# Sharing the quadrant moves of every pair between ScalarE and GpSimd, with 31 regular transfers in place of 39

## The chip, the cores and the metric

The kernel runs on one core of one Trainium2 chip. The metric is device time in microseconds (us) of that core. Most executions of one kernel agree within 0.3%, so every timed run stands beside runs of the kernel before on the same chip. Ratios are the mean time of one kernel's fast runs over that of the other's in the same rounds, so they are not quite the ratio of the medians quoted with them.

## The reference

```python
x:         16 x 512 x 1024 float32        weight: 1024 x 768 float32
add_value: 16 x 512 x 768  float32        scale:  0.1
out = (scale * np.matmul(x, weight) + add_value).astype(np.float32)
```

In tiles of 128 rows there are 64 tiles. One tile moves 4 KiB per partition of x in, 3 KiB of the add in and 3 KiB of the result out. With 3.1 MB of weights that is 87.03 MB in all.

## The kernel before

Tile t's rows are interleaved, so that 8 tiles of one partition are one contiguous run in memory: a transfer of 8 tiles of x is 128 rows of 32,768 bytes, one of the add or the result 128 rows of 24,576 bytes. SyncE issues all transfers in the order of a list. `x` loads tiles into 16 slots, `a` loads the add into 32 slots, `o` stores from those same slots, `w` loads weights; `l` and `r` are the two halves of tile 63.

```python
STREAM = [
    ("x", 0, 3), ("w", 0, 2), ("w", 2, 2), ("w", 4, 2), ("x", 3, 1), ("w", 6, 2),
    ("a", 0, 3), ("x", 4, 4), ("a", 3, 1), ("a", 4, 4), ("x", 8, 4), ("x", 12, 4),
    ("x", 16, 4), ("a", 8, 8), ("x", 20, 4), ("x", 24, 8), ("o", 0, 8), ("a", 16, 8),
    ("x", 32, 8), ("a", 24, 8), ("a", 32, 8), ("x", 40, 8), ("o", 8, 8), ("x", 48, 8),
    ("a", 40, 8), ("o", 16, 8), ("x", 56, 8), ("a", 48, 8), ("o", 24, 8), ("o", 32, 8),
    ("a", 56, 8), ("o", 40, 8), ("o", 48, 8), ("o", 56, 4), ("o", 60, 1), ("o", 61, 1),
    ("o", 62, 1), ("l", 63, 1), ("r", 63, 1),
]
```

x must be transposed for the product. The first 14 tiles and the last four are transposed by TensorE. A pair of the tiles in between is cast and moved between quadrants of 32 partitions in 16 small copies, and VectorE's stream transpose then finishes it. ScalarE does all 16 copies of one pair while GpSimd does those of the next; each has its own pool of two buffers.

```python
def move_pair(t0, a):                       # called for a = 0..3, four steps in a row
    act = t0 in MOVED_ACT
    if a == 0:
        if act:
            va = va_pool.tile([P, 2 * KC, 4, 64], bf16, tag="va")
        else:
            va = vp_pool.tile([P, 2 * KC, 4, 64], bf16, tag="vp")
        ...
    for b in range(4):
        move = nc.scalar.copy if act else nc.gpsimd.tensor_copy
        move(moved[t0][32 * b:32 * b + 32, :, a, :], src[32 * a:32 * a + 32, :, b, :])

def step():                                 # one tile
    ...
        for a in range(4):                  # in the middle of the tile's matmuls
            if in_pair.get(t + 8 - a) == t + 8 - a:
                move_pair(t + 8 - a, a)
    ...
    finish(t, BOTH[0], 0, N)                # VectorE: scale * product + add, into the add's slot
    if in_pair.get(t + 4) == t + 4:
        turn_moved(t + 4)                   # VectorE: stream transpose of a moved pair
```

An x slot is free for the next load only when its tile has been moved. And VectorE takes its work in program order.

Of the kernel before, what the change touches and what calls it, by code (L numbers as in the profile page):

```python
# [10 lines left out]

STREAM = [
    ("x", 0, 3), ("w", 0, 2), ("w", 2, 2), ("w", 4, 2), ("x", 3, 1), ("w", 6, 2),
    ("a", 0, 3), ("x", 4, 4), ("a", 3, 1), ("a", 4, 4), ("x", 8, 4), ("x", 12, 4),
    ("x", 16, 4), ("a", 8, 8), ("x", 20, 4), ("x", 24, 8), ("o", 0, 8), ("a", 16, 8),
    ("x", 32, 8), ("a", 24, 8), ("a", 32, 8), ("x", 40, 8), ("o", 8, 8), ("x", 48, 8),
    ("a", 40, 8), ("o", 16, 8), ("x", 56, 8), ("a", 48, 8), ("o", 24, 8), ("o", 32, 8),
    ("a", 56, 8), ("o", 40, 8), ("o", 48, 8), ("o", 56, 4), ("o", 60, 1), ("o", 61, 1),
    ("o", 62, 1), ("l", 63, 1), ("r", 63, 1),
]  # L20

X_SLOTS = 16
# [3 lines left out]
EARLY = 3  # L26



MOVED_ACT = [14, 18, 22, 26, 30, 34, 38, 42, 46, 50, 54, 58]  # L30
MOVED_POOL = [16, 20, 24, 28, 32, 36, 40, 44, 48, 52, 56]


@with_exitstack
def kernel(
# [8 lines left out]
    nc = tc.nc  # L44
    P = 128
    bf16 = mybir.dt.bfloat16
# [9 lines left out]
    KC = K // (2 * P)  # L56
# [8 lines left out]
    def rows(view, s, n):  # L65
        assert s // G == (s + n - 1) // G
        return view[:, s // G, s % G:s % G + n, :]


    w_v = weight.rearrange("(c p r) n -> p c r n", p=P, r=2)  # L70

    const = ctx.enter_context(tc.tile_pool(name="const", bufs=1))
    xb_pool = ctx.enter_context(tc.tile_pool(name="xb_pool", bufs=XB_BUFS))
    xt_pool = ctx.enter_context(tc.tile_pool(name="xt_pool", bufs=3))
    va_pool = ctx.enter_context(tc.tile_pool(name="va_pool", bufs=2))
    vp_pool = ctx.enter_context(tc.tile_pool(name="vp_pool", bufs=2))
    tp_pool = ctx.enter_context(
        tc.tile_pool(name="tp_pool", bufs=2, space=bass.MemoryType.PSUM))
    mm_pool = ctx.enter_context(
# [6 lines left out]
    ao = const.tile([P, A_SLOTS, N], fp32, name="ao")  # L86
    w_bf = const.tile([P, KJ, N], bf16, name="w_bf")

    xb_tiles, xt_tiles, mm_tiles, done = {}, {}, {}, {"cast": 0, "step": 0, "x": 0}
    in_pair = {t0 + i: t0 for t0 in MOVED_ACT + MOVED_POOL for i in range(2)}  # L90
    moved, cast_pairs = {}, set()

    def load_w(j, n):

        s = A_SLOTS - KJ + j
        if n == 1:
            nc.sync.dma_start(ao[:, s, :], w_v[:, j // 2, j % 2, :])
        else:
            nc.sync.dma_start(ao[:, s:s + 2, :], w_v[:, j // 2, :, :])  # L99
        for i in range(n):  # L100
            nc.vector.tensor_copy(w_bf[:, j + i, :], ao[:, s + i, :])  # L101

    def move_pair(t0, a):


        act = t0 in MOVED_ACT
        if a == 0:
            if act:
                va = va_pool.tile([P, 2 * KC, 4, 64], bf16, tag="va")
            else:  # L110
                va = vp_pool.tile([P, 2 * KC, 4, 64], bf16, tag="vp")
            moved[t0] = va
        k = t0 % X_SLOTS
        assert k + 1 < X_SLOTS
        src = xs[:, k:k + 2, :].rearrange("p i (c b k) -> p (i c) b k", b=4, k=64)
        for b in range(4):
            move = nc.scalar.copy if act else nc.gpsimd.tensor_copy
            move(moved[t0][32 * b:32 * b + 32, :, a, :], src[32 * a:32 * a + 32, :, b, :])  # L118
        if a == 3:
            cast_pairs.add(t0)  # L120

    def turn_moved(t0):
        xt = xt_pool.tile([P, 2, KC, P], fp32, tag="xt")
        for i in range(2):
            xt_tiles[t0 + i] = xt[:, i, :, :]
        nc.vector.transpose(  # L126
            xt.rearrange("p i c m -> p (i c m)"),
            moved.pop(t0).bitcast(fp32).rearrange("p c a k -> p (c a k)"))

    def cast_to(t):  # L130
        while done["cast"] <= t:
            i = done["cast"]
            if i in in_pair:
                assert in_pair[i] in cast_pairs
                done["cast"] += 1
                continue
            if len(xb_tiles) == XB_BUFS:
                break
            xb = xb_pool.tile([P, K], bf16, tag="xb")
            src = xs[:, i % X_SLOTS, :]  # L140
            if i < EARLY:
                nc.vector.tensor_copy(xb[:, 0:K // 2], src[:, 0:K // 2])  # L142
                other = nc.gpsimd.tensor_copy if i else nc.scalar.copy
                other(xb[:, K // 2:K], src[:, K // 2:K])  # L144
            else:
                nc.gpsimd.tensor_copy(xb, src)  # L146
            xb_tiles[i] = xb
            done["cast"] += 1

    def transpose(t, pieces=1):  # L150
        cast_to(t)

        pairs = xb_tiles.pop(t).bitcast(fp32)
        tp = tp_pool.tile([P, KC, P], fp32, tag="tp")
        for c in range(KC):
            nc.tensor.transpose(tp[:, c, :], pairs[:, c * P:(c + 1) * P], identity)  # L156
        if t % 2 == 0:
            xt = xt_pool.tile([P, 2, KC, P], fp32, tag="xt")
            for i in range(2):
                xt_tiles[t + i] = xt[:, i, :, :]  # L160
        q = KC // pieces
        evacuate = nc.scalar.copy if t <= EARLY or t > LAST_PAIR else nc.vector.tensor_copy
        for c in range(0, KC, q):
            evacuate(  # L164
                xt_tiles[t][:, c:c + q, :].bitcast(bf16), tp[:, c:c + q, :].bitcast(bf16))
# [5 lines left out]
    def product(t, j, cols):  # L171
        if (t, cols[0]) not in mm_tiles:
            mm = mm_pool.tile([P, 1024], fp32, tag="mm")
            for part in cols:
                mm_tiles[t, part] = mm
        for n0, n1 in cols:
            nc.tensor.matmul(  # L177
                mm_tiles[t, cols[0]][:, n0:n1], lhs(t, j), w_bf[:, j, n0:n1],
                start=(j == 0), stop=(j == KJ - 1))
# [3 lines left out]
    def finish(t, part, n0, n1):  # L183
        a = ao[:, t % A_SLOTS, n0:n1]
        nc.vector.scalar_tensor_tensor(  # L185
            a, mm_tiles[t, part][:, n0:n1], float(scale), a,
            op0=mybir.AluOpType.mult, op1=mybir.AluOpType.add)
# [27 lines left out]
                        op0=mybir.AluOpType.mult)  # L215
            done["step"] = EARLY

    LAST_PAIR = max(in_pair)
    EARLY_AT = A_SLOTS - KJ - EARLY

    def step():
        t = done["step"]
        if t < T - 1:
            for j in range(KJ):
                if j == KJ // 2:
                    if t + 1 not in in_pair:
                        transpose(t + 1)
                    cast_to(min(t + AHEAD, done["x"] - 1))
                    for a in range(4):
                        if in_pair.get(t + 8 - a) == t + 8 - a:  # L230
                            move_pair(t + 8 - a, a)
                product(t, j, BOTH)
            finish(t, BOTH[0], 0, N)
            if in_pair.get(t + 4) == t + 4:
                turn_moved(t + 4)
        else:
            for cols in BOTH:
                for j in range(KJ):
                    product(t, j, [cols])
                finish(t, cols, *cols)  # L240
        done["step"] += 1

    def added(t):
        assert done["step"] >= EARLY
        nc.vector.tensor_add(  # L245
            ao[:, t, :], ao[:, EARLY_AT + t, :], ao[:, t, :])

    for op, s, n in STREAM:
        last = s + n - 1
        if op == "w":  # L250
            load_w(s, n)
            head(op, s, n)
        elif op == "x":
            if last >= X_SLOTS:
                while done["cast"] <= last - X_SLOTS:
                    step()
            k = s % X_SLOTS
            nc.sync.dma_start(xs[:, k:k + n, :], rows(x_v, s, n))  # L258
            done["x"] = s + n
            if last < EARLY:  # L260
                head(op, s, n)
        elif op == "a":
            k = s % A_SLOTS
            nc.sync.dma_start(ao[:, k:k + n, :], rows(add_v, s, n))  # L264
            for t in range(s, min(s + n, EARLY)):
                added(t)
        else:
            while done["step"] <= last:
                step()
            k = s % A_SLOTS  # L270
            n0, n1 = {"o": (0, N), "l": (0, CUT), "r": (CUT, N)}[op]
            nc.sync.dma_start(rows(out_v, s, n)[:, :, n0:n1], ao[:, k:k + n, n0:n1])  # L272
# [35 lines left out]
```

## Time and profile before

| | before |
|---|---|
| time, median | 210.12 us (210.09 to 210.5, 3 runs) |
| span of the profiled run | 208.5 us |
| pairs moved, tiles transposed by TensorE | 23, 18 |

The DMA row of the page says whether the 16 DMA engines had work in each of 40 slices.

### The profile page before, as it was taken

The numbers are of one execution on the slowest core, as the hardware profiler recorded it, in microseconds if no ns is written. First come the engines' busy times: TensorE is split into PE (matmuls) and PEld (weight loads), VectorE is DVE, ScalarE is ACT, GpSimd is POOL, SyncE is SP. The second block draws the span as 40 slices with busy tenths as digits, with TensorE's granted clock in tenths as the row PEclk, the third lists the DMA queues.
The fourth block names the chain that finished last, engine by engine and source line by source line (L and its number), as shares of the span: only waits on it lengthen the run. The fifth ranks groups of instructions, "written<-read, shape, count | busy, mean of one in ns | idle before, by whom it ended". The sixth has DMA issues, their size and how long they took to land.

```text
span 208.5 us, 2886 instructions
## 1 busy us (share of the span) xinstructions
PE 181.6 (87%) x1096; PEld 110.7 (53%) x1096; DVE 101.3 (49%) x111; ACT 129.0 (62%) x206; POOL 124.3 (60%) x199
## 2 busy tenths in 40 slices
PE   0599399980899997999999999999999999989960
PEld 0455256650466664566666666666666666656630
DVE  0536535511466514855655555555553685233330
ACT  2423000499959798599999999999999900003210
POOL 1310524379898980999998899999999960001000
PEclk9999889996589999999999999999999999999997
DMA  6999999999999999999999999999999999999995
GB/s 236 415 428 440 413 429 434 421 450 406 454 418 448 407 429 462 404 443 420 442 434 413 461 418 424 420 429 437 421 434 424 432 439 424 429 418 439 429 394 214
DMA packets 5629, 87.21 MB, mean 418 GB/s; under 512 B 624, under 2 KB 752, under 8 KB 2032
## 3 DMA queue, kind: packets, MB, share of 16 engines
q1 hardware_dynamic: 5616, 87.03, 98.2%
q8 instruction: 8, 0.13, 0.3%
q14 instruction: 5, 0.04, 0.0%
HBM read 61.87 MB, written 25.17 MB: 417 GB/s over the span
## 4 chain that ended last, share of the span: by engine, by line
DMA 75%; ACT 9%; PE 7%; DVE 3%; SPq 1%; issue 1%; DVEq 0%
DMA out_dram<-ao 35%; DMA ao<-in_add_value_dram 22%; DMA xs<-in_x_dram 13%; ACT va L118 9%; PE mm L177 6%; DMA ao<-in_weight_dram 5%; DVE ao L185 2%; DVE xt L126 1%; PE tp L156 1%; SPq L258 1%; SPq L99 0%; SPq L264 0%; SPq L272 0%; DVEq L185 0%
## 5 line engine op out<-in xcount | busy, mean ns | idle before, releaser
L177 PE MATMUL mm<-w_bf,xt 128*128 128x256 bf16 (+1 forms) x1024 | 173.8, 331 | 8.8 <-DVE xt L164 6.6
L177 PEld LDWEIGHTS <-xt 128*128 128x128 bf16 x1024 | 101.3, 99 | 76.9 <-DVE xt L164 7.0
L118 ACT CAST va<-xs 32x512 bf16<-32x512 f32 x192 | 118.2, 616 | 28.8 <-DMA xs<-in_x_dram 19.1
L118 POOL CAST va<-xs 32x512 bf16<-32x512 f32 x176 | 106.8, 607 | 15.9 <-DVE xt L126 6.2
L185 DVE SCALAR_TENSOR_TENSOR ao<-mm,ao 128x768 f32<-128x768 f32 (+2 forms) x62 | 58.1, 942 | 78.1 <-PE mm L177 49.1
L146 POOL CAST xb<-xs 128x1024 bf16<-128x1024 f32 x15 | 15.2, 1040 | 43.4 <-PE tp L156 22.5
L164 ACT COPY xt<-tp 128x512 bf16<-128x512 bf16 (+1 forms) x11 | 8.2, 785 | 35.3 <-PE tp L156 35.3
L126 DVE STREAM_TRANSPOSE xt<-va 128x1024 f32<-128x1024 f32 x23 | 28.4, 1234 | 0.0
L156 PE MATMUL tp<-identity,xb 128*128 128x128 f32 x72 | 12.9, 314 | 11.2 <-DVE xb L142 7.4
L156 PEld LDWEIGHTS tp<-identity,xb 128*128 128x128 f32 x72 | 9.8, 161 | 13.7 <-issue 7.6
L164 DVE COPY xt<-tp 128x1024 bf16<-128x1024 bf16 x10 | 6.9, 686 | 10.1 <-PE tp L156 10.1
L101 DVE CAST w_bf<-ao 128x768 bf16<-128x768 f32 x8 | 4.1, 556 | 3.8 <-DMA ao<-in_weight_dram 3.8
L142 DVE CAST xb<-xs 128x512 bf16<-128x512 f32 x3 | 1.9, 696 | 6.8 <-DMA xs<-in_x_dram 6.8
L144 POOL CAST xb<-xs 128x512 bf16<-128x512 f32 x2 | 1.6, 834 | 5.5 <-DMA xs<-in_x_dram 5.5
L144 ACT CAST xb<-xs 128x512 bf16<-128x512 f32 x1 | 0.6, 618 | 4.8 <-DMA xs<-in_x_dram 4.8
L213 DVE TENSOR_SCALAR ao<-mm 128x768 f32<-128x768 f32 x2 | 1.8, 952 | 1.9 <-PE mm L177 1.9
L245 DVE TENSOR_TENSOR ao<-ao 128x768 f32<-128x768 f32 x3 | 2.7, 951 | 0.0
L144 ACT ACT_TABLE_LOAD x1 | 1.3, 1283 | 0.7 <-PEq L289 0.7
L210 ACT ACTIVATE ao<-mm 128x768 f32<-128x768 f32 x1 | 0.8, 817 | 0.0
masks.py:197 POOL MEMSET identity<- 128x128 f32 x1 | 0.2, 204 | 0.3 <-POOLq L289 0.3
masks.py:199 POOL TENSOR_SCALAR_AFFINE_SELECT identity<-identity 128x128 f32<-128x128 f32 x1 | 0.3, 292 | 0.1
L289 POOL MEMSET const-float32-0.0<- 128x1 f32 x1 | 0.1, 98 | 0.2 <-issue 0.2
(3 smaller groups left out, 0.3 us busy)
## 6 DMA issues: line engine op xcount, KB each, us to landing
ao<-in_add_value_dram SPq DMA_DIRECT2D x7, 3072.0 KB, 26.1
out_dram<-ao SPq DMA_DIRECT2D x7, 3072.0 KB, 23.9
xs<-in_x_dram SPq DMA_DIRECT2D x5, 4096.0 KB, 18.8
xs<-in_x_dram SPq DMA_DIRECT2D x5, 2048.0 KB, 26.6
ao<-in_weight_dram SPq DMA_DIRECT2D x4, 768.0 KB, 9.6
xs<-in_x_dram SPq DMA_DIRECT2D x1, 1536.0 KB, 6.1
ao<-in_add_value_dram SPq DMA_DIRECT2D x1, 1536.0 KB, 19.3
out_dram<-ao SPq DMA_DIRECT2D x1, 1536.0 KB, 12.9
```

The lines of the kernel that those rows point to most:

```text
L101: nc.vector.tensor_copy(w_bf[:, j + i, :], ao[:, s + i, :])
L118: move(moved[t0][32 * b:32 * b + 32, :, a, :], src[32 * a:32 * a + 32, :, b, :])
L126: nc.vector.transpose(xt.rearrange("p i c m -> p (i c m)"), moved.pop(t0).bitcast(fp32).rearrange("p c a k -> p (c a k)"))
L142: nc.vector.tensor_copy(xb[:, 0:K // 2], src[:, 0:K // 2])
L144: other(xb[:, K // 2:K], src[:, K // 2:K])
L146: nc.gpsimd.tensor_copy(xb, src)
L156: nc.tensor.transpose(tp[:, c, :], pairs[:, c * P:(c + 1) * P], identity)
L164: evacuate(xt_tiles[t][:, c:c + q, :].bitcast(bf16), tp[:, c:c + q, :].bitcast(bf16))
L177: nc.tensor.matmul(mm_tiles[t, cols[0]][:, n0:n1], lhs(t, j), w_bf[:, j, n0:n1], start=(j == 0), stop=(j == KJ - 1))
L185: nc.vector.scalar_tensor_tensor(a, mm_tiles[t, part][:, n0:n1], float(scale), a, op0=mybir.AluOpType.mult, op1=mybir.AluOpType.add)
L245: nc.vector.tensor_add(ao[:, t, :], ao[:, EARLY_AT + t, :], ao[:, t, :])
L258: nc.sync.dma_start(xs[:, k:k + n, :], rows(x_v, s, n))
```

## The change

Its intent: fewer and larger transfers in a regular order (31, in eights from tile 8 on), each issued well ahead; and to make that possible, moves with half the latency, shared by ScalarE and GpSimd within every pair from tile 14 on. The diff, cut to its core:

```diff
 STREAM = [
     ("x", 0, 3), ("w", 0, 2), ("w", 2, 2), ("w", 4, 2), ("x", 3, 1), ("w", 6, 2),
-    ("a", 0, 3), ("x", 4, 4), ("a", 3, 1), ... ("o", 56, 4), ("o", 60, 1), ("o", 61, 1),
-    ("o", 62, 1), ("l", 63, 1), ("r", 63, 1),
+    ("a", 0, 8), ("x", 4, 4), ("x", 8, 8), ("a", 8, 8), ("x", 16, 8), ("o", 0, 8),
+    ("a", 16, 8), ("x", 24, 8), ("a", 24, 8), ("o", 8, 8), ("x", 32, 8), ("a", 32, 8),
+    ("x", 40, 8), ("o", 16, 8), ("a", 40, 8), ("x", 48, 8), ("a", 48, 8), ("o", 24, 8),
+    ("x", 56, 8), ("o", 32, 8), ("a", 56, 8), ("o", 40, 8), ("o", 48, 8), ("o", 56, 6),
+    ("o", 62, 2),
 ]
-MOVED_ACT = [14, 18, 22, ... 58]
-MOVED_POOL = [16, 20, 24, ... 56]
+MOVED = [14, 16, 18, ... 60, 62]
-    vp_pool = ctx.enter_context(tc.tile_pool(name="vp_pool", bufs=2))
     ...
+    def move_pair(t0, half):
+        if half == 0:
+            va = va_pool.tile([P, 2 * KC, 4, 64], bf16, tag="va")
         for b in range(4):
+            for a, move in ((2 * half, nc.scalar.copy), (2 * half + 1, nc.gpsimd.tensor_copy)):
+                move(moved[t0][32 * b:32 * b + 32, :, a, :],
+                     src[32 * a:32 * a + 32, :, b, :])
     ...
-                    for a in range(4):
-                        if in_pair.get(t + 8 - a) == t + 8 - a:
-                            move_pair(t + 8 - a, a)
+                    for half in range(2):
+                        if in_pair.get(t + 6 - half) == t + 6 - half:
+                            move_pair(t + 6 - half, half)
```

## The prediction

> **What bounds the kernel now.** I read the page from the bottom of part 3 upwards: first what the transfers do, then how deep their queue is, and only then the engines.
>
> ```profile
> span 208.5 us, 2886 instructions
> PE 181.6 (87%) x1096; PEld 110.7 (53%) x1096; DVE 101.3 (49%) x111; ACT 129.0 (62%) x206; POOL 124.3 (60%) x199
> ...
> DMA  6999999999999999999999999999999999999995
> ...
> q1 hardware_dynamic: 5616, 87.03, 98.2%
> ...
> HBM read 61.87 MB, written 25.17 MB: 417 GB/s over the span
> ```
>
> The DMA row is 9 in 38 of 40 slices, and the queue that carries the data took 98.2% of 16 engines' span. The inputs and the output together are 87.03 MB; nothing is moved twice. So the kernel stands at the time that 87.03 MB need, plus a start and an end. The stretches say how much that is:
>
> ```profile
> 0.00:2.00 2.00, 0.00 (x0) 0.00 (x0) 0.00 (x0) 1.27 (x1) 0.70 (x6) 1.00 0.36 68
> 2.00:205.00 203.00, 181.63 (x1096) 110.67 (x1096) 101.26 (x111) 127.78 (x206) 123.61 (x193) 0.97 1.00 427
> 205.00:208.50 3.50, 0.00 (x0) 0.00 (x0) 0.00 (x0) 0.00 (x0) 0.00 (x0) 0.58 0.31 118
> ```
>
> The last two columns are DMA share and GB/s. From 2 to 205 us the share is 1.00 at 427 GB/s: no hole is left to fill. The records of single packets give the same: the first data packet starts at 1.75 us, the last ends at 207.27 us, and of these 205.5 us each of the 16 engines spent 204.7 us in packets (3275.9 us of packet time divided by 16). Idle in between: 0.8 us.
>
> The second reading is whether that queue was ever near empty:
>
> ```profile
> out_dram<-ao SPq DMA_DIRECT2D x7, 3072.0 KB, 23.9
> xs<-in_x_dram SPq DMA_DIRECT2D x5, 4096.0 KB, 18.8
> ```
>
> A 4 MiB load needs 9.8 us at 427 GB/s, and landed 18.8 us after its issue: it stood about 9 us behind others. Issue by issue (issue times from the timeline of the transfer queue, landings from the packets), the shortest backlog at an issue after the start was 5.6 us, at the load of tiles 48 to 55 issued at 116.08 us. The table of waits shows SyncE waiting 90.1 us for ScalarE's moves in 5 waits; with that backlog these waits cost no DMA time. The same holds for the chain that ended last: it gives 9% to ScalarE's moves, but they only delayed an issue whose data then stood in the queue.
>
> The engines follow. TensorE does a tile in 2.60 us (16 matmuls) and needs 0.44 us more where it transposes. Two tiles' traffic is 20 KiB per partition, 2.62 MB, or 6.1 us at 427 GB/s, against TensorE's 5.2 and 16 moves x 0.62 = 9.9 us of ScalarE per four tiles, which is 12.3 us of traffic. All have slack over the whole run.
>
> **What the Trainium skill says.** "DMA: Bandwidth & Descriptors", section "Where 436 GB/s comes from", puts the ceiling of a core's 16 engines at 435.2 GB/s. The trace agrees: packets of 24,576 and 32,768 bytes have medians of 0.912 and 1.213 us, so 8,192 bytes more take 0.301 us, 27.2 bytes per ns and engine, 435 GB/s on 16. The same section says that for loads from HBM about 358 binds; the trace disagrees with 427 over 203 us. "HBM Reference", section "Specifications (TRN2)", explains it: a core that streams alone measures about 425. Section "Why small descriptors are slow (HBM only)" of the first page names a fixed overhead per packet; here it is 0.912 us less 24,576/27.2 ns = 8 to 9 ns. "ScalarE: Activation LUTs", section "What ACT_TABLE_LOAD costs", has 186 ns + 0.833 ns per element, 612 ns for a 512-element move; the row of these moves has 616.
>
> **The change, part by part.**
>
> *Fewer, larger transfers.* Every transfer is 128 rows of one partition each, one packet a row. Before there are 39 transfers and 4,992 data packets, after 31 and 3,968. The bytes are the same. The gain is the fixed part: 1,024 packets x 8.7 ns / 16 = 0.56 us. Summing the packet medians instead gives 3,245 us before; after, by size in bytes, 128 of 4,096, 640 of 6,144, 128 of 12,288, 128 of 16,384, 128 of 18,432 (0.687 us, interpolated), 1,920 of 24,576 and 896 of 32,768 come to 3,234 us: 11 / 16 = 0.7 us. Eight transfers fewer are also 128 completion packets of 9 ns, 0.07 us. Sum: **0.7 us off the path that sets the end**. The weight pattern written as (r n) is no gain: its rows were already 6,144 bytes.
>
> *The moves.* Before, ScalarE does all 16 moves of one pair (9.9 us) while GpSimd does the next pair's. After, each does 8 of every pair (8 x 0.616 = 4.9 us and 8 x 0.607 = 4.9 us): same throughput, half the latency. Two more pairs, tiles 60 to 63, are moved too: 8 more moves on ScalarE, 24 more on GpSimd, 2 more stream transposes (1.23 us each) on VectorE, against 16 fewer TensorE transposes (4 x 0.44 = 1.8 us) and 4 ScalarE evictions of 1.0 us gone. None of it is on the bound; it only moves issue times.
>
> *Buffers and order.* One pool of two move buffers serves all pairs, so the moves of pair t wait for the stream transpose of pair t-4, after tile t-8 is finished. I worked the new stream through by hand, with queue time from the bytes (8 tiles of x 9.8 us, of a or o 7.4 us). Through the weights nothing differs: 15.1 us. Then queue ends: a0 22.3, x4 27.2, x8 37, a8 44, x16 54, o0 61, a16 69, x24 78, a24 86, o8 93, x32 103, a32 110, x40 120, o16 127, a40 135, x48 144, a48 152, o24 159, x56 169, o32 176, a56 184, o40 191, o48 198, o56 204, o62 206. Against these the issues:
> x16 needs tile 7's cast, about 31, queue end then 44; o0 needs tile 7 finished (x4 lands 4.4 us later than before, so about 45), queue end 54; x24 needs pair 14's moves, about 53, queue end 69; o8 needs tile 15, about 69, queue end 86; x32 needs pair 22's moves, 74, queue end 93; x40 needs pair 30's, 98, queue end 110; x48 needs pair 38's (x32 lands 103, four pairs x 4.96 us), 123, queue end 135; a48 needs o16 landed, 129, queue end 144; x56 needs pair 46's, 143, queue end 159; a56 needs o24 landed, 160, queue end 176. The smallest backlog is 9 us. That is more than the 5.6 us of before, and as nothing was lost at 5.6, nothing is gained by 9.
>
> *The end.* x56 lands near 170, four pairs of moves run to about 190, the add for tiles 56 to 63 lands near 185; tile 63 then starts near 195 and is finished by about 199 (before: 202.04). The last store, 768 KB, is issued there and stands behind o56 until 204, so the larger last piece costs nothing.
>
> **The rivals.** (1) *The queue runs dry in the new order.* For it: two shared move buffers in place of four, x4 behind a whole a0, and SyncE takes its waits in order, so one late x holds back all behind it. Against it: 9 us of backlog in my working. If a pair were 9 us late everywhere, some refill would leave a hole, perhaps 1 to 4 us in all: 210.5 to 213.5 us. (2) *The end becomes bound by compute.* The old tail came in single tiles and two halves; the new one stores the last two tiles at once. If tile 63 is finished after about 202, each us later shows in full; with the ScalarE chain 4 us late, 211 us. Against it: 1.8 us less TensorE work and a 3 us margin. (3) *The engines are relieved and the kernel gets much faster.* TensorE waits less around tiles 10 to 19, where before it stood for adds landing at 50.8 and 80.5; after, these land at 44 and 69. This speaks for earlier finishes, not for an earlier end: the 2:205 row has no DMA time to give. It would need over 435 GB/s to win 2%.
>
> **Range and chances.** Span before 208.5 us, time 210.12. Less 0.7 us for packets: 209.4 us. Idle at start (1.75 us) and after the last packet (1.2 us) should stay. A good case also gets back some of the 0.8 us idle: 208.7. A small hole of a us or so gives 210.3. Faster by over 2% (under 205.9) would beat the ceiling of the 16 engines: 0.02. Slower by over 2% (above 214.3) needs over 4 us of empty queue: 0.03. The rest, 0.95, is within 2%.
>
> **What would show it.** Right: 3,968 data packets and, with the completion packets, about 1,150 packets fewer than the 5,616 of before; DMA row still 9 in all but the first and last slice; rate from 2 to 203 us 427 to 430 GB/s; ScalarE and GpSimd busy a little more (about +1 us and +10 us, four casts of 1.04 us being gone as well), TensorE less by some 2 us; TensorE's and VectorE's wait for adds near tiles 10 and 16 gone, or moved to tile 56; landing of 4 MiB loads 18 us or more after issue. Wrong: a slice of the DMA row under 9 in the middle (rival 1, and the wait of SyncE just before it names the late engine), or a last store whose data starts more than 3 us after the end of the store ahead of it (rival 2), or a data rate that differs with the same packet sizes.

## The result, and the profile after

The change measured 210.34 us (210.13 to 210.79, 4 runs) against 210.28 us of the kernel before (4 runs): ratio 1.0005, interval 0.9985 to 1.0026. Two later sets of rounds gave 1.0027 and 1.0030 (below). So the time is the same within 2%, as forecast, but the 0.7 us did not come: it would be a ratio of 0.9967, which lies under all three intervals (their lower ends are 0.9985, 1.0009 and 1.0016). If anything 0.1 to 0.6 us were lost.

The page after, in the same rows as before (engines' busy time, DMA share of the slices, the data queue, and two rows of the issues, whose last column is the us from issue to landing):

```profile
span 209.0 us, 2845 instructions
PE 178.1 (85%) x1059; PEld 108.7 (52%) x1080; DVE 102.3 (49%) x113; ACT 129.9 (62%) x210; POOL 135.2 (65%) x219
...
DMA  6999999999999999999999999999999999999993
...
q1 hardware_dynamic: 4464, 87.03, 97.8%
...
xs<-in_x_dram SPq DMA_DIRECT2D x7, 4096.0 KB, 25.5
...
out_dram<-ao SPq DMA_DIRECT2D x7, 3072.0 KB, 27.1
```

The packets fell from 5,616 to 4,464, the bytes did not change, and the DMA row is still 9 to the last slice. A 4 MiB load now stands some 16 us in the queue instead of 9. (TensorE's row lacks 21 of 1,024 matmul records in all three profiles of this kernel. Two runs below that differ from it only in a few transfers, the swap and the halves, have them all, x1080, and show 180.5 and 180.1 us.)

The waits of VectorE, before and after (engine and line, what it waited for, us in total, times, longest):

```profile
DVE ao L185 <- PE mm L177: 49.1, 48, 2.1
DVE ao L185 <- DMA ao<-in_add_value_dram: 29.0, 5, 8.6
```

```profile
DVE xt L120 <- POOL va L111: 55.2, 22, 5.6
DVE ao L179 <- PE mm L171: 12.6, 16, 1.9
...
DVE ao L179 <- DMA ao<-in_add_value_dram: 4.4, 2, 2.3
```

The waits for late adds shrank from 29.0 to 4.4 us, and a new one took their place: 22 stream transposes wait for GpSimd. Eight moves of 0.608 us with some 0.04 us between them are 5.2 us a pair, which is just what TensorE needs for two tiles. Near the end this holds tiles back (VectorE's timeline; start, length, what it did, and in brackets the idle time before it):

```profile
176.73 1.25 DVE L120 STREAM_TRANSPOSE xt<-va 128x1024 f32<-128x1024 f32 x1 [5.00 <-POOL va L111]
177.90 1.78 DVE L179 SCALAR_TENSOR_TENSOR ao<-mm,ao 128x768 f32<-128x768 f32 x2
181.96 1.25 DVE L120 STREAM_TRANSPOSE xt<-va 128x1024 f32<-128x1024 f32 x1 [2.28 <-POOL va L111]
183.13 0.92 DVE L179 SCALAR_TENSOR_TENSOR ao<-mm,ao 128x768 f32<-128x768 f32 x1
```

The two `finish` at 177.90 are those of tiles 53 and 54, though tile 53's product was ready before 174 us: the transpose ahead of them waited 5.00 us for moves of x that had landed at 171 us. So the store of tiles 48 to 55 was issued only at 184.08 us, and those of 56 to 61 and 62 to 63 at 196.35 and 201.01 us.

### Where the time went, from the packet records

Summed over the packets of the data queue and divided by 16 engines, in us. "At medians" counts each packet at the median of its size; "excess" is what the packets took beyond it; "idle" is the rest from the first packet's start to the last packet's end, less what successive packets of one engine overlap (so it can be negative).

| profile | at medians | excess | idle | last packet ends |
|---|---|---|---|---|
| before | 203.13 | 1.61 | 0.78 | 207.27 |
| after, first | 202.38 | 1.98 | 1.66 | 207.77 |
| after, second | 202.41 | 1.96 | 1.92 | 208.04 |
| after, third | 202.42 | 1.88 | 1.45 | 207.50 |

The saving at medians is there, 0.7 us. It is given back in two places. The excess grew by 0.3 to 0.4 us, and its place is narrow: at the change from the last load ahead of the first store to that store (52 to 54 us), 11 to 18 packets of these 16 engines are slow by 0.15 to 1.6 us each. Summed over the packets there and divided by 16 this is 0.67, 0.39 and 0.60 us in the three profiles after, and 0.08 us before (at 62 us). And the idle grew by 0.7 to 1.1 us, nearly all of it after 200 us (before 1.03 us, after 1.79, 2.03 and 1.63 us).

Much of that growth is the engine that arrives last. Each transfer raises its semaphore by one for each of the 16 DMA engines (496 arrivals for the 31 transfers); the times of these arrivals, for the last store of each profile, are (us):

```
profile        first   median  15th    last     time of that run   time - last
before         205.17  206.53  207.45  207.59   210.28             2.69
after, first   204.95  206.43  207.29  208.11   210.79             2.68
after, second  205.21  206.37  207.10  208.37   211.06             2.69
after, third   204.75  206.36  207.24  207.83   210.51             2.68
```

The median engine is 0.10 to 0.17 us earlier after the change. The last engine is 0.2 to 0.8 us later, and the time is the last engine's arrival plus 2.7 us in every row (2.6 to 2.9 us in all fourteen profiles).

Each row is one execution. The first profile after was the slowest of its four runs (210.79 us, median 210.34), and runs of one kernel on one chip differ by 0.2 to 1.1 us, so single rows are compared with care; that the last engine did not get earlier rests on the timed runs too.

The overlap is worth a look, because it has a size. Matching each packet's start to the nearest end ahead of it (the records do not name the engine) gives 16 unbroken chains, and in them the next packet starts 3 to 4 ns before the record of the one ahead ends. Over the run that is 1.25 us per engine before and 0.99 us after, with fewer packets. So 0.25 of the 0.73 us saved at medians was time that two packets had shared; some 0.48 us was left, and the slow packets took 0.3 to 0.4 of it. That agrees with the chains, whose last packets end 0.11 to 0.25 us earlier in the mean, and with the 0.10 to 0.17 us of the median engine.

### The profile page after: what moved, and what is told of

It is laid out like the page before. It is cut to its first block, busy times and chain, and to the rows that moved or that the text cites. A ratio compares the mean times of both kernels' runs of the same rounds, so it can differ in the third digit from the quotient of the medians.

```text
span 209.0 us, 2845 instructions
## 1 busy us (share of the span) xinstructions
PE 178.1 (85%) x1059; PEld 108.7 (52%) x1080; DVE 102.3 (49%) x113; ACT 129.9 (62%) x210; POOL 135.2 (65%) x219
## 3 DMA queue, kind: packets, MB, share of 16 engines
q1 hardware_dynamic: 4464, 87.03, 97.8%
## 4 chain that ended last, share of the span: by engine, by line
DMA 64%; PE 15%; POOL 13%; SPq 2%; issue 2%; DVE 1%; POOLq 0%; DVEq 0%
DMA out_dram<-ao 28%; DMA xs<-in_x_dram 24%; PE mm L171 13%; DMA ao<-in_add_value_dram 12%; POOL va L111 12%; PE tp L150 2%; POOL xb L140 2%; SPq L94 1%; DVE ao L179 1%; SPq L251 1%; SPq L257 0%; POOLq L140 0%; DVEq L179 0%; SPq L265 0%; POOLq L111 0%
## 5 line engine op out<-in xcount | busy, mean ns | idle before, releaser
L171 PE MATMUL mm<-w_bf,xt 128*128 128x512 bf16 (+1 forms) x1003 | 171.6, 328 | 7.8 <-DVE ao L179 6.3
L111 ACT CAST va<-xs 32x512 bf16<-32x512 f32 x200 | 123.2, 616 | 47.4 <-DMA xs<-in_x_dram 44.9
L111 POOL CAST va<-xs 32x512 bf16<-32x512 f32 x200 | 121.7, 608 | 21.3 <-DMA xs<-in_x_dram 12.5
L179 DVE SCALAR_TENSOR_TENSOR ao<-mm,ao 128x768 f32<-128x768 f32 (+2 forms) x62 | 55.9, 925 | 17.0 <-PE mm L171 12.6
L120 DVE STREAM_TRANSPOSE xt<-va 128x1024 f32<-128x1024 f32 x25 | 31.1, 1244 | 55.3 <-POOL va L111 55.2
L140 POOL CAST xb<-xs 128x1024 bf16<-128x1024 f32 x11 | 11.2, 1043 | 29.7 <-DMA xs<-in_x_dram 25.5
L150 PE MATMUL tp<-identity,xb 128*128 128x128 f32 x56 | 10.2, 317 | 14.6 <-DVE xb L136 7.4
L150 PEld LDWEIGHTS tp<-identity,xb 128*128 128x128 f32 x56 | 7.7, 163 | 16.5 <-issue 7.4
L158 ACT COPY xt<-tp 128x512 bf16<-128x512 bf16 (+1 forms) x7 | 4.1, 655 | 8.7 <-PE tp L150 8.7
```

What stands on the lines that cost most here:

```text
L120: nc.vector.transpose(xt.rearrange("p i c m -> p (i c m)"), moved.pop(t0).bitcast(fp32).rearrange("p c a k -> p (c a k)"))
L140: nc.gpsimd.tensor_copy(xb, src)
L150: nc.tensor.transpose(tp[:, c, :], pairs[:, c * P:(c + 1) * P], identity)
L158: evacuate(xt_tiles[t][:, c:c + q, :].bitcast(bf16), tp[:, c:c + q, :].bitcast(bf16))
L171: nc.tensor.matmul(mm_tiles[t, cols[0]][:, n0:n1], lhs(t, j), w_bf[:, j, n0:n1], start=(j == 0), stop=(j == KJ - 1))
L179: nc.vector.scalar_tensor_tensor(a, mm_tiles[t, part][:, n0:n1], float(scale), a, op0=mybir.AluOpType.mult, op1=mybir.AluOpType.add)
```

## The experiments

Twelve runs, in four sets; a set shares its chip and its runs of the kernel before. At first I held **theory A**: the saving is real and the coarse last stores, which wait for tiles finished late, give it back. Its rivals are named in the expectations.

### The changed kernel again

No edit.

> The changed kernel once more, for the noise and for a second profile. Theory A (the packet saving of 0.7 us is real, the end gives it back): packet time over 16 engines at the sizes' medians again 202.4 us against 203.1 us of the kernel before, idle of the engines after 200 us again some 1.8 us against 1.0 us; ratio to before 0.998 to 1.001. Theory B (the first profile fell on an unlucky run, whose slow packets near 52 us cost 0.65 us; typical runs do gain 0.7 us): ratio 0.996 to 0.998, no slow packets near 52 us, idle at the end some 1.0 us.

211.01 us (6 runs) against 210.32 us (11 runs), ratio 1.0027 (1.0009 to 1.0045). Theory B falls: the slow packets near 52 us and the long idle at the end came again, so the first profile was not bad luck.

### The two parts, each alone

The first run has the new moves and the STREAM of before; the second has the old moves and the new STREAM. The edit of each is the list alone:

```diff
 # newmoves_oldstream: the changed kernel
-STREAM = [ 31 transfers ]
+STREAM = [ the 39 transfers of before ]
 # oldmoves_newstream: the kernel before
-STREAM = [ 39 transfers ]
+STREAM = [ the 31 transfers of the change ]
```

> The shared moves of every pair with the 39 transfers of before. Theory A: packet time that of before (203.1 us), tail in small pieces, so idle at the end near 1.0 us: ratio 0.999 to 1.001. A rival, theory C (the moves, now paced by GpSimd at 5.2 us a pair, cost time by finishing tiles late): ratio over 1.003 and SyncE issuing with a backlog near 0 somewhere.

> The moves of before with the 31 transfers of the change. Theory A: packet time 202.4 us, idle at the end as in the changed kernel if its size is due to the coarse last stores (ratio 0.998 to 1.001), or less if it is due to late tiles, which the moves of before do not have (then 0.996 to 0.998). Theory C: this one is faster than the changed kernel by 0.5 us or more.

The new moves alone: 218.00 us, ratio 1.0367 (1.0345 to 1.0390). The new transfers alone: 213.50 us, ratio 1.0156 (1.0129 to 1.0182). Neither was expected (theory C had even forecast the second to be faster than the changed kernel): each part alone loses what both together do not. Theory C named the moves, but its backlog near 0 came from the buffers, as shown below.

New moves, old transfers (the DMA and GB/s rows of the page, then waits of ScalarE and VectorE, each a view of its own):

```profile
DMA  7999999999999999999799889999999999999994
GB/s 248 409 425 442 411 435 430 442 432 426 445 423 420 432 405 432 409 432 421 274 454 320 362 291 467 391 353 438 465 401 430 429 427 432 436 417 432 414 409 168
```

```profile
ACT va L112 <- DVE xt L121: 28.5, 6, 11.2
```

```profile
DVE ao L180 <- DMA ao<-in_add_value_dram: 44.5, 6, 9.9
```

Slices 20, 22 and 24 fall to 274, 320 and 291 GB/s: the queue ran dry. The chain behind it reads backwards through the three views. VectorE waits 44.5 us for adds, which in the old order come late; behind these adds stand its stream transposes; they free the only two move buffers, for which ScalarE waits 28.5 us in all; without moves no x slot comes free. The loads of tiles 40 to 47 and 48 to 55 were issued at 103.87 and 124.77 us, with 1.8 and 0.3 us of work left on the slowest engine.

Old moves, new transfers:

```profile
DMA  6999999999899999999999999999999999999476
GB/s 242 412 458 409 437 421 465 413 414 483 364 437 429 441 414 415 435 440 455 407 424 463 412 426 427 441 434 400 441 454 421 424 429 432 418 435 437 181 314 281
```

```profile
DVE xt L125 <- POOL va L117: 51.0, 11, 7.9
```

Here the hole is at the end, 181 GB/s in slice 38. The new order lands the last x at 171 us, where before it landed at 156. A pair's moves take 10 us on one engine, so pairs 56 and 58 were ready near 181.5 us only, and the transposes of the last four tiles by TensorE followed. The store of tiles 56 to 61 was issued at 201.93 us, 1.5 us after the last arrival of everything ahead of it, and tile 63 was finished at 207.0 us, 6.0 us later than in the changed kernel. The run without pairs 60 and 62, below, is 1.7 us later in the same place; the other 4.3 us go with the moves that one engine does alone. So the new moves are what lets the regular order stand without that hole.

### The old last stores

```diff
-    ("o", 56, 6), ("o", 62, 2),
+    ("o", 56, 4), ("o", 60, 1), ("o", 61, 1), ("o", 62, 1), ("l", 63, 1), ("r", 63, 1),
```

> The changed kernel, only the last stores as before: 4, 1, 1, 1 tiles and two halves in place of 6 and 2 tiles. Packets cost 4 transfers x 128 x 8.7 ns / 16 = 0.28 us more. Theory A: idle at the end falls from 1.8 to about 1.0 us, so the sum is some 0.5 us faster than the changed kernel (ratio to before 0.996 to 0.999). Theory B: 0.2 to 0.3 us slower than the changed kernel.

211.09 us against 211.01 us of the changed kernel on the same chip (ratios 1.0029 and 1.0027). The idle after 200 us fell only to 1.58 us, and the last engine arrived at 208.25 us, median 206.59 us. Theory A in the form that I held falls: the shape of the last stores does not set the end. What is common to all rows is the last engine.

### Where do the slow packets come from?

The second set, on another chip, asks about the slow packets at 52 us, whether the loss of the new moves alone is due to the buffers, and what a packet costs.

```diff
 # new_swap: the add of tiles 16 to 23 ahead of the first store
-    ("x", 16, 8), ("o", 0, 8), ("a", 16, 8), ("x", 24, 8),
+    ("x", 16, 8), ("a", 16, 8), ("o", 0, 8), ("x", 24, 8),
```

> The changed kernel with the add of tiles 16 to 23 issued ahead of the first store instead of behind it. In four profiles with the new stream nearly all engines' packets are slow by 0.2 to 1.6 us near 52.5 us, at the end of the load of tiles 16 to 23, just ahead of the first store. Theory D (a load followed by the first store costs this): the slow packets move to some 60 us, the end of that add. Rival E (it is that load, or that moment): they stay at 52 to 53 us. Either way the ratio to before stays at 0.999 to 1.004; only if they vanish is the last engine some 0.5 to 1 us earlier.

```diff
 # new_x16halves
-    ("x", 16, 8), ("o", 0, 8),
+    ("x", 16, 4), ("x", 20, 4), ("o", 0, 8),
```

> The changed kernel with the load of tiles 16 to 23 in two transfers of 4 tiles, as before. Cost by packets 128 x 8.7 ns / 16 = 0.07 us. Theory E (the one 4 MiB load that follows the add of tiles 8 to 15 is the cause): no slow packets near 52.5 us, the sum of excess over the medians from 50 to 58 us under 0.1 us instead of 0.4 to 0.7, the last engine 0.5 to 1 us earlier, ratio 0.996 to 0.999. Theory D: slow packets stay, ratio 1.000 to 1.004.

The swap: 210.39 us, ratio 1.0009 (0.9997 to 1.0021). The slow packets are gone from 52 us and stand at 59 to 62 us instead, 0.50 us, at the end of the add that now comes before the first store. Theory D holds and E falls: it is the change from loading to the first store, not that load or that moment. The halves: 210.38 us, ratio 1.0006 (0.9992 to 1.0019); the slow packets stay, at 0.28 us, with packets of half the size. The changed kernel was not timed on this chip, so the two ratios are not to be ranked against its 1.0005 to 1.0030.

### The move buffers

```diff
 # newmoves_oldstream, and:
-    va_pool = ctx.enter_context(tc.tile_pool(name="va_pool", bufs=2))
+    va_pool = ctx.enter_context(tc.tile_pool(name="va_pool", bufs=4))
```

> The new moves with the 39 transfers of before lost 3.7% (3.6 us of empty queue between 58 and 150 us). Theory F (two move buffers make the moves, and with them the freeing of x slots and the next load, wait for a stream transpose that stands behind a late add): with four buffers, as many as before had in its two pools, the queue does not run dry; ratio 0.998 to 1.006. Rival G (six tiles ahead instead of eight, or GpSimd's pace of 5.2 us a pair, is what starves it): ratio stays over 1.025.

210.11 us against 210.07 us, ratio 0.9997 (0.9984 to 1.0010), and the same two rows of the page have no hole:

```profile
DMA  6999999999999999999999999999999999999995
GB/s 238 416 428 440 410 429 437 418 450 412 445 428 428 417 429 442 431 423 434 447 421 426 434 445 425 410 436 426 453 425 407 442 429 429 425 432 434 422 399 217
```

Theory F holds. Of the 7.7 us lost (218.00 against 210.32 us), all came, within the noise, from going from four move buffers to two; in this order of transfers the new moves themselves cost and gain nothing.

### What a packet costs

```diff
-    ao = const.tile([P, A_SLOTS, N], fp32, name="ao")
+    ao = const.tile([P, A_SLOTS, N + 4], fp32, name="ao")[:, :, 0:N]
```

with the weights' load written for rows that are no longer contiguous.

> The changed kernel with four elements of padding behind each tile's row of the add and output buffer, so that each transfer there goes in packets of 3,072 bytes: 14,720 more data packets, nothing else changed in order or number of transfers. The packet term as the prediction had it, 8.7 ns x 14,720 / 16 = 8.0 us: 218 to 220 us, ratio 1.035 to 1.045, packet time up by 8 us. If packets' fixed cost is hidden (rival), ratio under 1.01.

215.02 us, ratio 1.0229 (1.0214 to 1.0244): under the 218 to 220 expected, far over the rival's 1.01.

```profile
q1 hardware_dynamic: 19184, 87.03, 99.7%
```

The packets' summed time rose by 8.3 us over 16 engines (from 204.4 to 212.6 us), as expected. But the span rose only by 4.2 us (213.2 us against a mean of 209.0 of the three profiles of the changed kernel): an engine's packets overlap by the 3 to 4 ns of above, 4.15 us per engine in this run, and the idle of the table above comes out at minus 2.4 us. So a packet more costs about 4.2 us x 16 / 14,720 = 4.6 ns of span, half of the 9.0 ns by which its record makes the sum longer (8.3 us x 16 / 14,720), and close to the prediction's 8.7 ns less the overlap. The changed kernel was profiled on other chips; by the times on this one the run is 4.95 us above the kernel before, so 4.3 to 4.9 us above the changed one, which gives 4.7 to 5.3 ns. The first store has 0.04 us of slow packets here, the least of all runs.

### The place of the first store, and late tiles

The third set has the changed kernel on the same chip.

> The changed kernel a third time, as the partner of the next run on the same chip. Slow packets at 52 to 54 us again (0.4 to 0.7 us over 16 engines), ratio to before 1.000 to 1.004.

210.52 us against 210.01 us, ratio 1.0030 (1.0016 to 1.0044).

```diff
 # new_o0later
-    ("x", 16, 8), ("o", 0, 8), ("a", 16, 8), ("x", 24, 8), ("a", 24, 8),
+    ("x", 16, 8), ("a", 16, 8), ("x", 24, 8), ("o", 0, 8), ("a", 24, 8),
```

> The changed kernel with the first store behind the load of tiles 24 to 31, as before had it (order x16, a16, x24, o0). Before paid 0.08 us of slow packets for that first change from load to store, the changed kernel 0.4 to 0.7 us, and 0.5 us when the store stood behind the add at 61 us. Theory H (it costs where nearly all engines are in step, which they no longer are by 70 us after the second fetch of instructions): under 0.15 us at some 71 us, the last engine 0.5 to 1 us earlier than in the changed kernel on the same chip, ratio 0.996 to 0.999. Rival I (the first store in the new stream always pays): 0.4 us or more near 71 us, ratio as the changed kernel's.

210.62 us, ratio 1.0022 (1.0009 to 1.0034), not separable from 1.0030. The slow packets moved once more, to 68 to 71 us, and take 0.44 us, though by then two engines are out of step as they were before the change. My theory H falls; rival I is right that the first store pays in this stream wherever it stands.

```diff
 # new_no6062: pairs 60 and 62 not moved, their tiles transposed by TensorE
-MOVED = [14, ... 56, 58, 60, 62]
+MOVED = [14, ... 56, 58]
-        evacuate = nc.scalar.copy if t <= EARLY else nc.vector.tensor_copy
+        evacuate = nc.scalar.copy if t <= EARLY or t >= 60 else nc.vector.tensor_copy
```

> The changed kernel with the last two pairs, tiles 60 to 63, transposed by TensorE as before, so that the last tiles do not wait for GpSimd's moves at 5.2 us a pair. If late tiles at the end set the time (the stores of tiles 56 to 61 and 62 to 63 issued at 196 and 201 us), the last tile is finished 1 to 3 us earlier or not at all later and the ratio falls by 0.002 to 0.004 against the changed kernel. If the last DMA engine sets it, whose queue was never empty, the ratio is that of the changed kernel within 0.001.

210.52 us, ratio 1.0024 (1.0011 to 1.0036). That is the second of the two outcomes, and with the stores not earlier but later: tile 63 was finished at 202.7 us instead of 201.0, so the last store came 1.8 us later than in the changed kernel (202.77 us), and the time did not grow. The first engine's arrival went from about 205.0 to 206.28 us, but the last engine arrived at 208.11 us as in the first profile after. The engines that were ahead waited for the store; the one that was behind did not. At this size late tiles are paid out of the lead of the 15 other engines.

### The old front with the regular rest

A last run takes the order of before up to the first store and the add behind it, then the regular order, with four move buffers.

```diff
-    ("a", 0, 8), ("x", 4, 4), ("x", 8, 8), ("a", 8, 8), ("x", 16, 8), ("o", 0, 8),
-    ("a", 16, 8), ("x", 24, 8), ("a", 24, 8), ...
+    ("a", 0, 3), ("x", 4, 4), ("a", 3, 1), ("a", 4, 4), ("x", 8, 4), ("x", 12, 4),
+    ("x", 16, 4), ("a", 8, 8), ("x", 20, 4), ("x", 24, 8), ("o", 0, 8), ("a", 16, 8),
+    ("a", 24, 8), ...
```

> The transfers of before up to the first store and the add behind it, from there on the regular order of the change, with the shared moves and four move buffers. 36 transfers, so 384 packets fewer than before. The first store has cost 0.44 to 0.67 us of slow packets in every profile of the new stream, wherever it stood, and about 0.1 us in every one of the old stream. Theory J (it goes with what is issued ahead of the first store): under 0.2 us here, last DMA engine done by 207.5 us, ratio 0.997 to 1.000. Rival K (it goes with something else, for instance chance): 0.4 us or more, ratio 1.001 to 1.004.

210.20 us against 210.13 us, ratio 1.0002 (0.9988 to 1.0016). The slow packets at the first store are down to 0.10 us and the last engine arrived at 207.43 us, both as theory J has it; the ratio lies at the edge of both expectations, and its interval holds the changed kernel's 1.0005 as well. The run also differs from the changed kernel by five more transfers and two more move buffers. (The expectation's "0.44 to 0.67 us" overlooks 0.39 us in the second profile after and 0.28 us in the halves.) It is no version that beats the kernel before; none of the twelve is.

The lag of the last engine behind the median one, at the two loads ahead of the first store and at the last store of all (us):

```
                            one transfer earlier   last load or add     last store
                                                   before first store   of all
before                      1.46                   1.87                 1.06
old order, four buffers     1.53                   1.96                 0.96
old front                   1.55                   1.82                 1.00
after, three profiles       1.57, 1.48, 1.68       2.73, 2.52, 2.68     1.68, 2.01, 1.47
swap                        1.49                   2.57                 1.22
first store later           1.58                   2.23                 0.97
halves                      1.35                   2.25                 0.72
```

One engine is already 1.3 us or more behind by 38 us in each of these profiles, just after the first of the eight fetches of instructions (16,384 bytes, 1.06 us in the records before and after), which take a share of these same engines; the next packet of that engine is some 0.5 us slow as well. In the new stream the first store then adds about 1 us (0.65 us where it stands later) to the lag of the last engine, in the old order and the old front 0.3 to 0.4 us. In the second profile after, one engine can be followed through the run by the matching above: it took the fetch at 35.6 us, had the slowest packet at the first store (1.30 us over the median, at 53.0 us) and was the last of all at 208.04 us.

But the last column does not follow the middle one. The lag shrinks on the way, and in the swap, the later store and the halves it ended at 0.7 to 1.2 us, with the last engine at 207.50, 207.27 and 207.16 us, no later than before (207.59 us). These three profiles were the fastest runs of their sets (210.18, 209.97 and 209.77 us against medians of 210.39, 210.62 and 210.38 us), so they do not clear the first store either. That its slow packets are what makes the end late is argued here, not shown.

## Why the prediction was wrong

The kind of result was right and its size wrong: 209.4 us was forecast in a range of 208.7 to 210.3 us, and 210.34 us came, with 0.1 to 0.6 us more than before in place of 0.7 us less.

- **Bound by the transfers: right.** The DMA row stayed at 9, 427 GB/s from 2 to 205 us in both profiles. Relieving engines gained nothing, so rival 3 fell as argued.
- **Packets: the records right, the worth too high.** The time at medians fell by 0.71 to 0.75 us, as summed. But a packet's fixed part is not all on the path: 3 to 4 ns of it overlap with the packet ahead, and with 14,720 more packets the span grew by some 5 ns a packet, not 8.7. By that rate 1,024 packets are 0.3 us, by the records less the overlap 0.5 us; both are estimates.
- **The step that failed: "Sum: 0.7 us off the path that sets the end."** It divides a sum over packets by 16, which treats the 16 engines as one, and the range kept the 0.8 us of idle between the first and the last packet, or less. The idle at the start (1.75 us) and after the last packet (1.2 us) did stay. In between, 0.25 us of the saving was overlap, 0.27 to 0.37 us came back as slow packets, and the idle grew from 0.78 to 1.45, 1.66 and 1.92 us. The median engine gained only 0.10 to 0.17 us, and the kernel ends when the last engine arrives: that one came 0.2 to 0.8 us later, 1.5 to 2.0 us behind the median at the last store, before 1.1 us. The working by hand had the end of the last store at 206 us; the median engine arrived at 206.36 to 206.43 us, the last at 207.83 to 208.37 us.
- **Why the last engine fell behind: open in part.** In all three profiles the first store's slow packets, 0.4 to 0.7 us where before had 0.08, go with a step of about 1 us in the last engine's lag. Moving the store moved them; the front of the old order had only 0.10 us of them. How much of the loss at the end they make is not shown, since three profiles with a step of 0.65 to 1.1 us (swap, halves, later store) ended no later than before.
- **The end: mis-sized, and forgiven.** I expected tile 63 to be finished by about 199 us; it was 201.0. The working left out that VectorE's transposes wait in order, which held the finish of tile 53 by 5 us, and GpSimd's pace of 5.2 us a pair. The run with the last store at 202.77 us showed that this was not what set the time.
- **Smallest backlog 9 us: wrong.** Measured as the 5.6 us of before was, on the slowest engine, it was 4.1 us at the store of tiles 56 to 61; on the engines ahead that store's data started 0.85 us after its issue. (The 5.6 us itself leaves out the last two half stores of before, some 4.7 us.) Rival 1, the queue running dry for want of buffers, did not come in the combination, but came at full size in the old order with two buffers (7.7 us) and, at the end, with the old moves (3.2 us). I had taken the moves as harmless ("it only moves issue times"); true of both parts together, not of either alone with its buffers.
- **Engine times: right.** ScalarE +0.9 us, GpSimd +10.9 us, TensorE down by 1.1 and 1.5 us, not quite 2, in the two nearest profiles with all records (swap and halves); 1,152 packets fewer; the wait for adds moved to tile 56. A slip without weight: a win of 2% would need some 432 to 434 GB/s by the prediction's own terms, not over 435.

What stays open, besides the weight of the first store at the end: why it disturbs the loads ahead of it so much more in the new front than in the old one. It does so wherever it stands in the new stream, less with smaller load packets (0.28 us) and hardly with 3,072-byte packets of adds and stores (0.04 us). It was not bisected further, and a rival, that the spread at the end varies by chance from run to run, is not excluded by one profile per run.

## What to carry to other kernels

When the DMA row is full from end to end, look for the time in the engine that arrives last, not in the mean: per-transfer arrival times of the 16 engines show it, and here one late engine ate a saving that the mean confirmed. Changes of buffers, latency and transfer order belong together: test each half alone, because two halves that lost 1.6 and 3.7% alone lost next to nothing together, and the half that loses tells which buffer or wait holds the other up.

## What the Trainium skill lacked or had wrong

- "DMA: Bandwidth & Descriptors", section "Where 436 GB/s comes from": it lets about 358 GB/s bind for transfers with HBM, without saying that this is for two cores at once, though the page's own measurements just above have 425 for a core alone. A core alone kept 427 GB/s over 203 us here, before and after; "HBM Reference" has this right.
- "DMA: Bandwidth & Descriptors", section "Why small descriptors are slow (HBM only)": it has a fixed overhead per packet, but not that successive packets of one engine overlap in the records, here by 3 to 4 ns. 14,720 more packets added 8.3 us of packet time per engine and only 4.2 us of span, so the records are not to be summed.
- None of the pages that I read has the cost of a change from loads to the first store: 0.39 to 0.67 us of slow packets over 16 engines in the changed kernel's profiles, 0.08 us before, with the last engine's lag growing by about 1 us.
- None of the pages that I read has a figure for the spread of the 16 engines at the end: the time was the last engine's arrival plus 2.7 us in all profiles of the first table of arrivals, while the median engine arrived 1.1 to 2.0 us earlier. Nor for what a fetch of instructions takes from the data: 16,384 bytes took an engine 0.93 to 1.10 us in the profile before, and its next packet was some 0.5 us slow after the first fetch.
